# Modulation weights in two halves of longer rows, x transposed by a diagonal of its statistic, and a new order for the start

## The chip, the cores and the metric

The kernel runs on one core of one Trainium2 chip. Its time is the device time of one execution in microseconds (us); the time before is the median of three runs. The profile is that of one more execution.

## The reference, cut to what matters

One layer of a hybrid encoder works on 1024 prompt rows and 32 sample rows of width 1024. The change touches only how the layer begins: the modulation vectors, the normalised and modulated input h, and the first product of h with the weights w_in, whose first 512 columns are u.

```python
def layer(x, c, w_mod, b_mod, g_norm, w_in, ...):
    mod = silu(c) @ w_mod + b_mod                     # 1024 x 3072 weights
    shift, scale, gate = split(mod, 3)
    h = rms_norm(x, g_norm) * (1.0 + scale) + shift   # rsqrt(mean(x*x) + eps) per row
    z = h @ w_in
    u, zs, q, k, v, za, qi, ki, wi, gm = split(z, offs)
    # branch A: state space model over u; branch B: top-k sparse attention
    # merge with sigmoid gates, w_o, gate, residual, and a last rms_norm
```

## The kernel before, in words

The 1056 rows form three groups (0, 1, 2) of 256, 384 and 416 rows, and these are nine row tiles of up to 128 rows (indices 0 and 1; 2 to 4; 5 to 8, of which 8 holds the 32 sample rows). The width of 1024 is eight blocks of 128, the index k. The matrix multiply wants h transposed, that is, k on the partitions, and in two parts, hH and hL, a rounded high part and the rest. A weight has two parts too, wh and wl, and a product is three matmuls (`mm3`, lines 271 to 273): wh by hH, wh by hL, wl by hH.

The start of the kernel is written out by hand in the string `START`. Its tokens are steps, and each engine runs its instructions in the order in which the tokens issue them. What the tokens are:

- `sq i`, `ss i`, `sc i`: for row tile i, the squares and their sum on ACT (L214), the statistic rstd by DVE and POOL (L218, L219), and the scaling of the whole 128 x 1024 tile by rstd on DVE (`xscale`, L223).
- `mm j h`: block j (256 columns) of scale (h = 0) or shift (h = 1) of w_mod, multiplied with the activated c on PE into `pmrow` (`mod_mm`, L286). The eight k go to four strips of 32 partitions, two k to a strip.
- `row j h`: `pmrow` copied to `mrow` by ACT (L291). `co j h`: PE turns the row into columns in `pmod`, and sums the four strips by a selecting matrix (`mod_cols`, L296). `ap j`: three small DVE steps make scale and shift, `scl` and `sh`, for k = 2j and 2j + 1 (L302 to L304).
- `xt g k`: PE transposes block k of group g, one transposition for a row tile, into a bank of PSUM (`xtrans`, L231). Two banks take turns. `hf g k`: ACT applies `scl` and `sh` (L237, L239). `sp g k`: DVE makes hH and hL (L77, L78).
- `wl`: the parts of the u weights of a quarter q (128 columns): q 0 by ACT and DVE (L259, L264), q 1 by POOL in four pieces (L263, L264). `ub q g k`: the three matmuls of `mm3` for quarter q, group g, block k (`ublock`, the tile named pss in the trace). `ue`: the finished u goes to SBUF by ACT.
- `ld..`: loads that SP issues at this place. `aN`: N steps of a list of small DVE work for the state space model, which waits for free moments.

SP issues all large loads in order on one queue. Before, that is: row tiles 0 to 2, blocks 00 and 01 of w_mod, u weights of q 0, blocks 10 and 11, u weights of q 1, row tiles 3 to 5, the four other blocks of w_mod, row tiles 6 to 8, and then the weights of the next stage. A block of w_mod is 1 MiB and lies in HBM in rows of 1 KiB, a quarter of the u weights is 512 KiB in rows of 512 B, a row tile 512 KiB in rows of 4 KiB.

After the last `ub`, `ssm_consts` (L529, L533) makes the constants of the state space model. From there a planner with fixed costs lays out the jobs (tile pz) and the model's steps; it does not depend on measured time.

Of the kernel before, what the change touches and what calls it, by code (L numbers as in the profile page):

```python
# [7 lines left out]
F32 = mybir.dt.float32  # L8
# [4 lines left out]
ALU = mybir.AluOpType  # L13
# [3 lines left out]
T, TS, D = 1024, 32, 1024  # L17
# [4 lines left out]
KT = 8  # L22
# [8 lines left out]
WB = 5  # L31
# [14 lines left out]
MR, ML, YS, YW, HI, HG, JO, SF = (), 1, 10, 15, 0, 0, 8, (2, 2, 2, 1)  # L46
C_U, C_ZS, C_Q, C_K, C_V, C_ZA, C_QI, C_KI, C_GM = 0, 512, 1024, 1536, 2048, 2560, 3072, 3584, 3656
START = """
    sq0 ss0 sq1 sc0 ss1 sq2 sc1 ss2 sc2 mm00 srow ldw21 a13 xt00 row00 xt01 co00 mm01 ldw30 row01 wl00 co01
    ap0 mm10 ldw31 a2 hf00 row10 xt02 sp00 hf01 co10 sp01 xt03 mm11 ldx67 a6 wl10 ub000 row11 co11 sq3 ub100  # L50
    ap1 ub001 a1 ub101 hf02 ss3 a1 hf03 sp02 sq4 sp03 ub002 ub102 sq5 ss4 ub003 sc3 ub103 sc4 mm20 ldx8 ldz
    ss5 row20 a2 co20 sc5 a5 mm21 xt10 row21 xt11 hf10 co21 hf11 ap2 xt12 sp10 xt13 hf12 mm30 hf13 xt04 sp11
    row30 ub010 hf04 co30 sp12 xt05 xt14 hf05 ub110 sp13 hf14 mm31 sp04 xt15 row31 xt06 hf15 ub011 sp05 co31
    sq6 xt07 ap3 ub111 ub012 sp14 hf06 ub112 hf07 xt16 sp15 ub013 sq7 xt17 sp06 ub113 up hf16 ub004 sp07
    ub104 hf17 ub014 sp16 sq8 ub114 sp17 ub005 zs ub105 ss6 ub015 ss7 ss8 ub115 ub006 ub106 sc6 ub016 ub116
    sc7 ub007 sc8 ub107 ue00 ub017 ue10 a5 xt20 ue01 xt21 ub117 hf20 ue11 sp20 hf21 xt22 a1 ub020 hf22 xt23
    sp21 ub120 hf23 xt24 sp22 ub021 ub121 hf24 sp23 xt25 ub022 hf25 sp24 xt26 ub122 hf26 ub023 sp25 xt27
    ub123 sp26 hf27 ub024 ub124 sp27 ub025 ub125 ub026 ub126 ub027 ub127 ue02 ue12
    """
# [1 line left out]
GROW = [[n for g_, _, n in ROWS if g_ == g] for g in range(3)]  # L61


def body(nc, tc, I, O, dbg=None):
# [3 lines left out]
    te, ve, se, ge, sp = nc.tensor, nc.vector, nc.scalar, nc.gpsimd, nc.sync  # L68
# [88 lines left out]
    sc2 = cst.tile([128, 2, 8], F32)  # L157
# [3 lines left out]
    scP = cst.tile([128, 8, 32], F32, name="scP")  # L161
# [7 lines left out]
    bmod = pcol[:, 8:32]  # L169
# [5 lines left out]
    srow = pp.tile([80, 128], F32)  # L175
# [11 lines left out]
    pa = stA.enter_context(tc.tile_pool(name="pa", bufs=2, side="right", reuse_waits="tile"))  # L187
    scl = cst.tile([128, 8, 2], F32)
    sh = cst.tile([128, 8, 2], F32)
    nhalf = cst.tile([128, 9], F32)  # L190
    ge.memset(nhalf, -0.5)
    ss = cst.tile([128, 9], F32)
    rstd = cst.tile([128, 9], F32)
    XG, XW = {}, []

    def xload(i):
        g, r, n = ROWS[i]
        if i < 2:
            xt = stg.tile([128, D], F32, name="xt", tag="stg")
        elif i < 5:  # L200
            xt = XH[i // 4][:, D * (i == 3):D * (i == 3) + D]
        elif i == 5:
            xt = pa.tile([128, D], F32, name="xt", bufs=1)
        else:
            if i % 2 == 0:
                XW.append(pa.tile([128, 2, D], F32, name="xw", tag="wm", bufs=WB))
            xt = XW[-1][:, i % 2]
        load_rows(xt, g, r, n, sp)
        XG.setdefault(g, []).append(xt)

# [7 lines left out]
        ve.tensor_scalar(ss[:n, i:i + 1], ss[:n, i:i + 1], 1.0 / D, EPS, op0=ALU.mult, op1=ALU.add)  # L218
        ge.tensor_tensor(rstd[:n, i:i + 1], ss[:n, i:i + 1], nhalf[:n, i:i + 1], op=ALU.pow)  # L219

    def xscale(i):
        g, r, n = ROWS[i]
        ve.tensor_scalar_mul(XG[g][r][:n], XG[g][r][:n], rstd[:n, i:i + 1])  # L223

    PX, HX = {}, {}

    def xtrans(g, k):
        px = ps_z("px")
        PX[g, k] = px
        for r, n in enumerate(GROW[g]):  # L230
            te.transpose(px[:, r * 128:r * 128 + n], XG[g][r][:n, k * 128:(k + 1) * 128], idf[:n, :n])  # L231
# [16 lines left out]
    def wload(src, kt, n, pool=None):  # L248
        raw = (pool or wst).tile([128, kt, n], F32, tag="raw", name="raw", bufs=2)
        sp.dma_start(raw, src.rearrange("(k p) e -> p k e", p=128))  # L250
        return raw
# [21 lines left out]
        te.matmul(ps, wl, xh, start=False, stop=last)  # L273


    sel2 = pa.tile([128, 2], F32, name="sel2", bufs=1)
    WM, MR_ = {}, {}

    def mod_load(j, h):
        wm = WM[j, h] = pa.tile([128, 8, 256], F32, name="wm", tag="wm", bufs=WB)  # L280
        c = (1024, 0)[h] + 256 * j
        sp.dma_start(wm, w_mod[:, c:c + 256].rearrange("(k p) e -> p k e", p=128))

    def mod_mm(j, h):
        for k in range(8):
            te.matmul(pmrow[32 * (k % 4):32 * (k % 4) + 32, 256 * h:256 * h + 256], scP[:, k], WM[j, h][:, k],  # L286
                      start=k < 4, stop=k >= 4)

    def mod_row(j, h):
        MR_[j, h] = pa.tile([128, 256], F32, name="mrow", bufs=2)  # L290
        se.copy(MR_[j, h], pmrow[:, 256 * h:256 * h + 256])  # L291

    def mod_cols(j, h):
        for i in range(2):
            ch = (8, 0)[h] + 2 * j + i
            te.matmul(pmod[:, 2 * ch:2 * ch + 2], MR_[j, h][:, 128 * i:128 * i + 128], sel2, start=True, stop=True)  # L296

    def mod_apply(j):
        kk = slice(2 * j, 2 * j + 2)
        ks = slice(8 + 2 * j, 10 + 2 * j)  # L300
        bc2 = lambda ap: ap.unsqueeze(2).to_broadcast([128, 2, 2])
        ve.tensor_tensor(scl[:, kk], pm[:, ks], bc2(bmod[:, ks]), op=ALU.add)  # L302
        ve.tensor_tensor(scl[:, kk], scl[:, kk], bc2(gcol[:, kk]), op=ALU.mult)
        ve.tensor_tensor(sh[:, kk], pm[:, kk], bc2(bmod[:, kk]), op=ALU.add)  # L304

    scol = cst.tile([128, 5, 16], F32)
    are, aim, h0r, h0i, ldc = (scol[:, k] for k in range(5))
# [13 lines left out]
    now, ve = ve, Later(ve, todo)  # L321
# [149 lines left out]
    for k in range(7):  # L471
        n = 1 << k
# [39 lines left out]
    ve = now  # L512
# [62 lines left out]
    class Stream:  # L575
        STEP = 0.483

# [173 lines left out]
    mod_load(0, 0)
    mod_load(0, 1)
    uload(0)
    mod_load(1, 0)
    mod_load(1, 1)
    uload(1)
    for i in range(3, 6):
        xload(i)
    mod_load(2, 0)
    ve.tensor_add(sel2, idf[:, 0:2], idf[:, 32:34])  # L760
    for j in (64, 96):
        ve.tensor_add(sel2, sel2, idf[:, j:j + 2])
# [435 lines left out]
    for k in range(9):  # L1198
        n = 128 if k < 8 else 32
# [3 lines left out]
        o = (k % 4) * 72  # L1203
# [10 lines left out]
    for j in range(4):  # L1214
# [3 lines left out]
        for i in range(2, 9):  # L1218
            t0, m, k0, nk = (128 * i - B0[1], 128, 0, 128 * (i + 1)) if i < 8 else (T - B0[1], 32, 1024, 544)
            for e in range(2):  # L1220
                h = 2 * j + e
# [4 lines left out]
                for a in range(nb):  # L1226
                    c = slice(k0 + a * w_, k0 + (a + 1) * w_)
# [627 lines left out]
    ss2 = wo2.tile([128, 3, 9], F32, name="ss2")  # L1855
# [33 lines left out]
    for rows in ((0, 1, 2), (8,), (3,), (4,), (5,), (6,), (LAST,)):  # L1889
        xts = {}  # L1890
        for hcol in range(2):
            for i in rows:
                n = 128 if i < 8 else 32
# [3 lines left out]
                xt = xts[i]  # L1897
# [63 lines left out]
```

## Time and profile before

| | |
|---|---|
| median of three runs | 1007.07 us (1004.39 to 1008.39) |
| the profiled execution | 1005.85 us, its span 1003.9 us |
| PE (matmul) busy | 961.5 us, 96% of the span |
| DVE, ACT, POOL busy | 763.8, 525.2 and 234.3 us |
| loaded and stored | 124.24 MB, 124 GB/s over the span |

PE stands for the matrix engine, PEld for its weight loads, DVE for the vector engine, ACT for the scalar engine, POOL for GpSimd and SP for the engine that issues the loads. A row of the timeline gives the start, the duration and the engine, the line of the kernel, the tile that is written and those that are read, the shape and a count, and in square brackets how long the engine sat idle before it and what ended that. A row with a count (x16) is merged from several instructions that follow one another. Matmuls overlap, so what one costs is read from start to start. In the table by stages PEclk is the clock that was granted to the matrix engine, 1.00 being full speed.

### The profile page before, as it was taken

Reading aid. Unit: us, or ns where it says so; the run is one execution under the profiler, and the core shown is the slowest. Engines: PE = TensorE matmul, PEld = TensorE weight load, DVE = VectorE, ACT = ScalarE, POOL = GpSimd, SP = SyncE. Lnnn points to the kernel's source line nnn. Section 1 sums busy time; section 2 is a strip of 40 time slices with the busy share of each in tenths; the row PEclk is TensorE's granted clock in tenths of the full one; section 3 lists DMA queues with packets and bytes.
Section 4 is the critical chain, followed back from the end, with each engine's and each line's share of the span. In section 5 each row is a group of like instructions: output and inputs, shape, how many; then the busy total and the mean of one; then the engine's idle time right before and its main releaser. Section 6 shows DMA issues by size and latency. Waiting matters only on the chain. (4 is left out here: it accounts for less than half of the span.)

```text
span 1003.9 us, 16913 instructions
## 1 busy us (share of the span) xinstructions
PE 961.5 (96%) x6034; PEld 898.6 (90%) x6034; DVE 763.8 (76%) x1747; ACT 525.2 (52%) x1126; POOL 234.3 (23%) x443
## 2 busy tenths in 40 slices
PE   4999999999999999999999989999999999999997
PEld 2789999999898898998999979899898989998786
DVE  4669979994776878889999976676678786885543
ACT  3642234433655656858897266565576564443111
POOL 2202400000000024343323633333222222430000
PEclk8899999999999999999999999999999999999999
DMA  9922425437485222323323431322229503553311
GB/s 314 293 79 91 138 69 136 116 94 197 172 256 157 64 64 64 106 75 107 104 89 91 160 94 54 90 83 85 86 65 304 191 23 108 185 197 109 116 63 63
DMA packets 134255, 124.24 MB, mean 124 GB/s; under 512 B 20256, under 2 KB 114932, under 8 KB 134172
## 3 DMA queue, kind: packets, MB, share of 16 engines
q1 hardware_dynamic: 133232, 122.62, 40.1%
q8 instruction: 47, 0.77, 0.3%
q10 hardware_dynamic: 780, 0.52, 0.2%
q14 instruction: 36, 0.29, 0.1%
q0 software_dynamic: 160, 0.03, 0.0%
HBM read 87.74 MB, written 34.83 MB: 122 GB/s over the span
## 5 line engine op out<-in xcount | busy, mean ns | idle before, releaser
L271 PE MATMUL pz<-hH,wh 128*128 128x384 f32 (+4 forms) x744 | 253.1, 340 | 2.7 <-ACT tg L713 2.0
L272 PE MATMUL pz<-hL,wh 128*128 128x384 f32 (+4 forms) x744 | 244.9, 329 | 0.0
L273 PE MATMUL pz<-hH,wl 128*128 128x384 f32 (+4 forms) x744 | 244.9, 329 | 0.0
L264 POOL TENSOR_TENSOR wl<-raw,wh 128x256 fp32r<-128x256 f32 (+1 forms) x180 | 134.8, 778 | 121.4 <-ACT wh L259 111.0
L271 PEld LDWEIGHTS pz<-hH,wh 128*128 128x128 f32 (+1 forms) x744 | 139.4, 187 | 7.8 <-ACT tg L713 2.3
L272 PEld LDWEIGHTS pz<-hL,wh 128*128 128x128 f32 (+1 forms) x744 | 138.9, 187 | 1.7
L273 PEld LDWEIGHTS pz<-hH,wl 128*128 128x128 f32 (+1 forms) x744 | 138.6, 186 | 1.3
L1568 ACT ACTIVATE junkb<-sco,thr 128x768 bf16<-128x768 f32 (+3 forms) x128 | 96.7, 756 | 31.3 <-DVE thr L1650 20.5
L1570 DVE TENSOR_SCALAR_CACHE_REDUCE junk<-sco,thr 128x1024 bf16<-128x1024 f32 (+2 forms) x96 | 105.4, 1098 | 2.2
L271 PE MATMUL pss<-hH,wh 128*128 128x256 f32 (+2 forms) x304 | 97.8, 322 | 0.7 <-ACT tg L713 0.5
L272 PE MATMUL pss<-hL,wh 128*128 128x256 f32 (+2 forms) x304 | 95.8, 315 | 0.0
L273 PE MATMUL pss<-hH,wl 128*128 128x256 f32 (+2 forms) x304 | 95.5, 314 | 0.0
L263 POOL CAST wh<-raw 128x256 fp32r<-128x256 f32 x88 | 38.1, 473 | 178.2 <-PE pz L272 108.9
L1499 ACT CAST PH<-pt 128x512 fp32r<-128x512 f32 (+2 forms) x96 | 43.1, 483 | 37.6 <-PE pt L1497 34.1
L271 PEld LDWEIGHTS pss<-hH,wh 128*128 128x128 f32 x304 | 58.6, 193 | 3.6 <-issue 2.1
L1500 DVE TENSOR_TENSOR PL<-pt,PH 128x512 fp32r<-128x512 f32 (+2 forms) x96 | 50.4, 552 | 14.6 <-ACT PH L1499 13.7
L272 PEld LDWEIGHTS pss<-hL,wh 128*128 128x128 f32 x304 | 58.2, 191 | 0.3 <-DVE hL L78 0.2
L273 PEld LDWEIGHTS pss<-hH,wl 128*128 128x128 f32 x304 | 58.2, 192 | 0.0
L1236 DVE SCALAR_TENSOR_TENSOR sco<-rl,wi,sco 128x384 f32<-128x384 f32 (+6 forms) x49 | 46.8, 963 | 13.8 <-ACT rl L1231 12.6
L1231 ACT ACTIVATE rl<-pss 128x384 f32<-128x384 f32 (+6 forms) x56 | 40.9, 739 | 27.1 <-PE pss L1229 21.5
L1417 ACT ACTIVATE Sm<-Sm,mx 128x128 f32<-128x128 f32 (+8 forms) x68 | 52.7, 775 | 0.9 <-DVE mx L1410 0.8
L1932 PE MATMUL psm<-o,mL 128*128 128x512 f32 (+1 forms) x136 | 52.0, 382 | 0.0
(403 smaller groups left out, 2167.7 us busy)
## 6 DMA issues: line engine op xcount, KB each, us to landing
raw<-in_w_in SPq DMA_DIRECT2D x44, 512.0 KB
thD<-tg SPq DMA_DIRECT2D x16, 528.0 KB
wm<-in_w_mod SPq DMA_DIRECT2D x8, 1024.0 KB
m<-thD SPq DMA_DIRECT2D x8, 528.0 KB
tgl<-thD SPq DMA_DIRECT2D x8, 528.0 KB
rraw<-in_w_mod SPq DMA_DIRECT2D x4, 1024.0 KB
kd<-kd SPq DMA_DIRECT2D x32, 128.0 KB
xo<-in_x_prompt SPq DMA_DIRECT2D x8, 512.0 KB
```

Of the source, the lines that this page charges most:

```text
L264: leng.tensor_sub(wl[:, c], raw[:, c], f32(wh[:, c]))
L271: te.matmul(ps, wh, xh, start=first, stop=False)
L272: te.matmul(ps, wh, xl, start=False, stop=False)
L273: te.matmul(ps, wl, xh, start=False, stop=last)
L1231: se.activation(rl[:m, :nk].rearrange("p (b c) -> p b c", c=w_), pv, AF.Relu)
L1236: ve.scalar_tensor_tensor(sco[i][:m, :nk], rl[:m, :nk], w, sco[i][:m, :nk], op0=ALU.mult, op1=ALU.add)
L1417: se.activation(P, P, AF.Exp, scale=-1.0, bias=self.mx, accum_out=self.rs)
L1499: se.copy(PH[:, b0:b1_, oc], src)
L1500: ve.tensor_sub(PL[:, b0:b1_, oc], src, f32(PH[:, b0:b1_, oc]))
L1568: se.activation(junkb[:m, :nk], x[:m], AF.Sign, bias=t, accum_out=cnt[:m, k:k + 1])
L1570: ve.tensor_scalar(junk[:m, :nk], x[:m], t, None, op0=ALU.is_lt, op1=ALU.add, accum_out=cnt[:m, k:k + 1])
L1932: te.matmul(ps, ml, wh, start=False, stop=last)
```

## The change

- The columns of scale and shift are loaded in two halves instead of four quarters. A half (h) holds 512 columns of shift and the same 512 of scale, so that it serves four blocks k. It comes in four pieces (i), each of two k, by two loads with rows of 2 KiB in HBM. `mm h i` multiplies a piece: four matmuls over 512 columns (before, eight over 256), shift and scale of two k in the four strips. `row h`, `co h` and `ap h` then stand once for a half: two copies of 512 columns, two times four products with a selecting matrix of four columns (`sel4`), two times three DVE steps.
- x is no longer scaled. DVE makes for each row tile a 128 x 128 diagonal matrix of rstd, `dg i`, and PE multiplies block k of the row tile by it, a float32 matmul that transposes and scales at once, where a transposition by the identity stood. In group 0 one `xt` does two k, into the halves of one bank.
- The u weights of both quarters come in one load with rows of 1 KiB, into a buffer of the modulation weights. Row tiles 5 and 6 share a buffer, and 7 and 8.
- The loads stand in another order: row tiles 0 and 1, the first half of w_mod, the u weights, row tiles 2 to 4, the second half, row tiles 5 to 8.
- `START` is written anew. `mm1 i`, the products of the second half, stand among the other steps.

```diff
-    sq0 ss0 sq1 sc0 ss1 sq2 sc1 ss2 sc2 mm00 srow ldw21 a13 xt00 row00 xt01 co00 mm01 ldw30 row01 wl00 co01
...
+    sq0 ss0 sq1 dg0 ss1 dg1 mm00 srow ldw10 a13 xt00 mm01 ldw11 xt02 mm02 ldw12 mm03 ldw13 row0 co0 ap0 wl00 wl10 ldx56
...
-    def xscale(i):
+    DG = {}
+
+    def xdiag(i):
         g, r, n = ROWS[i]
-        ve.tensor_scalar_mul(XG[g][r][:n], XG[g][r][:n], rstd[:n, i:i + 1])
+        DG[g, r] = pa.tile([128, 128], F32, name="dg", bufs=5)
+        ve.tensor_scalar_mul(DG[g, r][:n, :n], idf[:n, :n], rstd[:n, i:i + 1])
...
     def xtrans(g, k):
-        px = ps_z("px")
-        PX[g, k] = px
-        for r, n in enumerate(GROW[g]):
-            te.transpose(px[:, r * 128:r * 128 + n], XG[g][r][:n, k * 128:(k + 1) * 128], idf[:n, :n])
+        pb = ps_z("px")
+        for j in range(2 if g == 0 else 1):
+            px = PX[g, k + j] = pb[:, 256 * j:]
+            for r, n in enumerate(GROW[g]):
+                te.matmul(px[:, r * 128:r * 128 + n], XG[g][r][:n, (k + j) * 128:(k + j + 1) * 128], DG[g, r][:n, :n],
+                          start=True, stop=True)
...
+    def mod_load(h, i):
+        wm = WM[h, i] = pa.tile([128, 2, 2, 512], F32, name="wm", tag="wm", bufs=WB)
+        for k in range(2):
+            sp.dma_start(wm[:, k], w_mod[256 * i + 128 * k:256 * i + 128 * k + 128, 0:2048]
+                         .rearrange("p (c a e) -> p c a e", c=2, a=2)[:, :, h])
+
+    def mod_mm(h, i):
+        for k in range(2):
+            for c in range(2):
+                o = 32 * (2 * k + c)
+                te.matmul(pmrow[o:o + 32, :], scP[:, 2 * i + k], WM[h, i][:, k, c], start=i == 0, stop=i == 3)
...
+    def uload():
+        t = pa.tile([128, KT, 256], F32, name="wm", tag="wm", bufs=WB)
+        sp.dma_start(t, w_in[:, C_U:C_U + 256].rearrange("(k p) e -> p k e", p=128))
...
+    xload(0)
+    xload(1)
+    for i in range(4):
+        mod_load(0, i)
+    uload()
+    for i in range(2, 5):
+        xload(i)
```

How the order of the instructions changes, at three places. First PE, from the first product with w_mod to the first blocks of u. Before:

```order
L286 MATMUL pmrow<-wm,scP 32x256 x8
L733 MATMUL pmod<-idf,srow 128x80
L231 MATMUL px<-idf,xt 128x128 x4
L296 MATMUL pmod<-sel_137,mrow 128x2 x2
L286 MATMUL pmrow<-wm,scP 32x256 x8
L296 MATMUL pmod<-sel_137,mrow 128x2 x2
L286 MATMUL pmrow<-wm,scP 32x256 x8
L231 MATMUL px<-idf,xt 128x128 x2
L296 MATMUL pmod<-sel_137,mrow 128x2 x2
L231 MATMUL px<-idf,xt 128x128 x2
L286 MATMUL pmrow<-wm,scP 32x256 x8
L271 MATMUL pss<-hH_84,wh 128x256
```

Four products of 1 MiB stand ahead of the first block of u here, with three of their turns into columns (pmod) between them; hH_84 is the high part of group 0. The same place now, with dg for the diagonals:

```order
L291 MATMUL pmrow<-wm,scP 32x512 x4
L740 MATMUL pmod<-idf,srow 128x80
L232 MATMUL px<-dg,xt 128x128 x4
L291 MATMUL pmrow<-wm,scP 32x512 x4
L232 MATMUL px<-dg,xt 128x128 x4
L291 MATMUL pmrow<-wm,scP 32x512 x8
L300 MATMUL pmod<-sel_137,mrow 128x4 x4
L273 MATMUL pss<-hH_84,wh 128x256
```

Again four products of 1 MiB come first, and the turn into columns stands once behind them all. Second PE, from the last product with w_mod on, where hH_82 is the high part of group 1. Before:

```order
L286 MATMUL pmrow<-wm,scP 32x256 x8
L231 MATMUL px<-idf,xh 128x128 x3
L231 MATMUL px<-idf,xt 128x128 x2
L271 MATMUL pss<-hH_82,wh 128x384
L272 MATMUL pss<-hL_83,wh 128x384
L273 MATMUL pss<-hH_82,wl 128x384
L296 MATMUL pmod<-sel_137,mrow 128x2 x2
L231 MATMUL px<-idf,xt 128x128 x2
```

And now:

```order
L291 MATMUL pmrow<-wm,scP 32x512 x4
L232 MATMUL px<-dg,xt 128x128 x8
L300 MATMUL pmod<-sel_137,mrow 128x4 x4
L273 MATMUL pss<-hH_82,wh 128x384
L274 MATMUL pss<-hL_83,wh 128x384
L275 MATMUL pss<-hH_82,wl 128x384
```

All four blocks k = 4 to 7 of group 0 are now transposed behind the last product, and one more block of group 1 (for q 1) stands between the turn into columns and the first block of group 0 that needs it. Third ACT, from the first copy of the modulation row on; wm in the second row is the load of the u weights. Now:

```order
L295 COPY mrow<-pmrow 128x512
L261 CAST wh<-wm 128x1024
L239 ACTIVATE hf<-px,sh,scl 128x256 x2
L211 ACTIVATE sq,ss<-xh 128x1024 x2
L239 ACTIVATE hf<-px,sh,scl 128x256
L211 ACTIVATE sq,ss<-xh 128x1024
L239 ACTIVATE hf<-px,sh,scl 128x256
```

The squares of row tiles 2 and 3 stand ahead of the third `hf`, that of tile 4 ahead of the fourth. Behind the start the orders of both kernels differ by swaps alone: single steps of the state space model stand some rows later or earlier among the jobs.

More of the change, by code (lines that the diff above doesn't have):

```diff
@@ L48 @@
 START = """
-    sq0 ss0 sq1 sc0 ss1 sq2 sc1 ss2 sc2 mm00 srow ldw21 a13 xt00 row00 xt01 co00 mm01 ldw30 row01 wl00 co01
[L50 to L56, printed above, removed]
+    sq0 ss0 sq1 dg0 ss1 dg1 mm00 srow ldw10 a13 xt00 mm01 ldw11 xt02 mm02 ldw12 mm03 ldw13 row0 co0 ap0 wl00 wl10 ldx56
+    hf00 sp00 hf01 sp01 ub000 sq2 ss2 ub001 sq3 hf02 sp02 ss3 sq4 hf03 sp03 ss4 dg2 dg3 dg4 ub100 ub101 mm10 ldx78 ldz
+    ub002 ub102 ub003 ub103 a6 xt10 hf10 sp10 xt11 hf11 sp11 mm11 xt12 hf12 sp12 ub010 ub110 mm12 xt13 hf13 sp13 ub011
+    ub111 ub012 ub112 a14 sq5 ss5 mm13 row1 xt04 sq6 ss6 xt06 co1 ub013 ub113 ap1 hf04 sp04 sq7 ss7 hf05 sp05 ub004 ub104
+    hf06 sp06 xt14 ub005 ub105 dg5 dg6 hf07 sp07 xt15 ub006 ub106 hf14 sp14 ub007 ub107 sq8 ss8 xt16 hf15 sp15 ub014 ub114
+    xt17 hf16 sp16 dg7 dg8 ub015 ub115 hf17 sp17 xt20 ub016 ub116 up zs ue00 ue10 xt21 ub017 ub117 hf20 sp20 ue01
+    hf21 ue11 xt22 a1 ub020 hf22 xt23
     sp21 ub120 hf23 xt24 sp22 ub021 ub121 hf24 sp23 xt25 ub022 hf25 sp24 xt26 ub122 hf26 ub023 sp25 xt27
@@ L201, in xload @@
             xt = XH[i // 4][:, D * (i == 3):D * (i == 3) + D]
-        elif i == 5:
-            xt = pa.tile([128, D], F32, name="xt", bufs=1)
         else:
-            if i % 2 == 0:
+            if i % 2 == 1:
                 XW.append(pa.tile([128, 2, D], F32, name="xw", tag="wm", bufs=WB))
-            xt = XW[-1][:, i % 2]
+            xt = XW[-1][:, 1 - i % 2]
         load_rows(xt, g, r, n, sp)
@@ L273, in mm3 @@
         te.matmul(ps, wl, xh, start=False, stop=last)
-    sel2 = pa.tile([128, 2], F32, name="sel2", bufs=1)
+    sel4 = pa.tile([128, 4], F32, name="sel4", bufs=1)
     WM, MR_ = {}, {}
[L279 to L302, printed above, removed]
+    def mod_load(h, i):
[3 more added lines that the diff above has]
+                         .rearrange("p (c a e) -> p c a e", c=2, a=2)[:, :, h])
@@ new lines, in mod_mm, with mod_row, mod_cols @@
+    def mod_mm(h, i):
[3 more added lines that the diff above has]
+                te.matmul(pmrow[o:o + 32, :], scP[:, 2 * i + k], WM[h, i][:, k, c], start=i == 0, stop=i == 3)
+    def mod_row(h):
+        MR_[h] = pa.tile([128, 512], F32, name="mrow", bufs=1)
+        se.copy(MR_[h], pmrow)
+    def mod_cols(h):
+        for i in range(4):
+            k = 4 * h + i
+            te.matmul(pmod[:, 4 * k:4 * k + 4], MR_[h][:, 128 * i:128 * i + 128], sel4, start=True, stop=True)
@@ L303, in mod_apply @@
+    def mod_apply(h):
+        kk = slice(4 * h, 4 * h + 4)
+        ks = slice(8 + 4 * h, 12 + 4 * h)
+        bc2 = lambda ap: ap.unsqueeze(2).to_broadcast([128, 4, 2])
+        ve.tensor_tensor(scl[:, kk], pm[:, kk, 1], bc2(bmod[:, ks]), op=ALU.add)
         ve.tensor_tensor(scl[:, kk], scl[:, kk], bc2(gcol[:, kk]), op=ALU.mult)
-        ve.tensor_tensor(sh[:, kk], pm[:, kk], bc2(bmod[:, kk]), op=ALU.add)
+        ve.tensor_tensor(sh[:, kk], pm[:, kk, 0], bc2(bmod[:, kk]), op=ALU.add)
     scol = cst.tile([128, 5, 16], F32)
@@ L724, in body @@
     raw = {}
-    def uload(q):
-        raw[q] = wload(w_in[:, C_U + 128 * q:C_U + 128 * q + 128], KT, 128)
+    def uload():
+        t = pa.tile([128, KT, 256], F32, name="wm", tag="wm", bufs=WB)
+        sp.dma_start(t, w_in[:, C_U:C_U + 256].rearrange("(k p) e -> p k e", p=128))
+        for q in range(2):
+            raw[q] = t[:, :, 128 * q:128 * q + 128]
     def uparts(q):
@@ L747, in load @@
             f()
-    for i in range(3):
-        xload(i)
[L751 to L762, printed above, removed]
+    xload(0)
+    xload(1)
+    for i in range(4):
+        mod_load(0, i)
+    uload()
+    for i in range(2, 5):
+        xload(i)
+    for c in range(2):
+        ve.tensor_add(sel4[:, 2 * c:2 * c + 2], idf[:, 32 * c:32 * c + 2], idf[:, 64 + 32 * c:66 + 32 * c])
     ve.memset(dl, 0.0)
     pmod, pmrow = ps_t("pmod"), ps_t("pmrow")
-    pm = pmod[:, 0:32].rearrange("p (k s) -> p k s", s=2)
-    STEP = dict(sq=xsquare, ss=xrstd, sc=xscale, mm=mod_mm, row=mod_row, co=mod_cols, ap=mod_apply, xt=xtrans,
+    pm = pmod[:, 0:32].rearrange("p (k c s) -> p k c s", c=2, s=2)
+    STEP = dict(sq=xsquare, ss=xrstd, dg=xdiag, mm=mod_mm, row=mod_row, co=mod_cols, ap=mod_apply, xt=xtrans,
                 hf=xmod, sp=xsplit, wl=lambda q, _: uparts(q), ub=ublock, srow=srows, zs=lambda: Z.split(0), up=utiles,
@@ L780, in body @@
             STEP[n](*(int(c) for c in t[len(n):]))
-        if t == "wl00":
+        if t == "mm00":
             ssm_shifts()
```

## The prediction

> **What bounds the kernel now.** I read the table by stages first, then PE's timeline of the start, then the rows of ACT and DVE that stand between two steps of PE. From the table of stages (length, busy time and instruction count of PE, PEld, DVE, ACT and POOL, then the granted clock, the DMA share and GB/s):
>
> ```profile
> core 0: us, PE busy (x) PEld busy (x) DVE busy (x) ACT busy (x) POOL busy (x), PEclk, DMA share, GB/s
> 6.64:18.97 12.33, 5.64 (x47) 3.59 (x47) 7.57 (x28) 4.07 (x8) 2.34 (x4) 0.97 1.10 344
> 14.00:16.00 2.00, 1.88 (x22) 1.20 (x20) 1.69 (x10) 0.06 (x1) 0.00 (x0) 1.00 1.15 316
> 32.00:34.00 2.00, 1.44 (x20) 0.78 (x12) 1.36 (x7) 0.37 (x1) 0.34 (x1) 1.00 1.09 348
> 38.00:40.00 2.00, 2.00 (x27) 1.50 (x19) 1.90 (x6) 1.37 (x3) 0.00 (x0) 1.00 1.08 390
> 18.10:31.75 13.65, 12.69 (x68) 8.82 (x68) 7.96 (x31) 6.04 (x12) 5.93 (x10) 0.50 1.09 356
> 41.06:69.16 28.10, 28.09 (x181) 24.91 (x181) 17.84 (x48) 16.37 (x34) 2.44 (x6) 1.00 0.40 73
> 71.00:130.00 59.00, 59.00 (x372) 58.88 (x373) 50.64 (x190) 14.75 (x28) 17.60 (x19) 1.00 0.43 127
> ```
>
> The start has two halves. Up to about 41 us the loads run without a gap at 316 to 390 GB/s, by the length of their rows (316 where the u weights with rows of 512 B are among them, 348 with rows of 1 KiB alone, 390 where row tiles with 4 KiB come in), and PE waits for them; from 18.10 to 31.75 its clock is at half. From 41.06 on PE is busy for 28.09 of 28.10 us, and for 59.00 of 59.00 us after it. So what PE has left to do when the last block of w_mod is there sets when the start ends, and a delay there is carried on one for one. PE's timeline gives the marks and the prices:
>
> ```profile
> 18.97 1.94 PE L286 MATMUL pmrow<-wm,scP 128*32 128x256 f32 x16 [1.99 <-DMA wm<-in_w_mod]
> ...
> 24.79 0.58 PE L271 MATMUL pss<-hH,wh 128*128 128x256 f32 x1
> ...
> 30.57 0.41 PE L272 MATMUL pss<-hL,wh 128*128 128x256 f32 x1
> 30.78 0.41 PE L273 MATMUL pss<-hH,wl 128*128 128x256 f32 x1
> ...
> 34.34 1.07 PE L286 MATMUL pmrow<-wm,scP 128*32 128x256 f32 x16 [0.40 <-DMA wm<-in_w_mod]
> 35.34 0.88 PE L231 MATMUL px<-idf,xh 128*128 128x128 f32 x6
> ...
> 39.49 0.50 PE L296 MATMUL pmod<-sel,mrow 128*128 128x2 f32 x4
> 39.85 0.42 PE L231 MATMUL px<-idf,xt 128*128 128x128 f32 x2
> ...
> 41.06 1.07 PE L286 MATMUL pmrow<-wm,scP 128*32 128x256 f32 x16
> ...
> 45.41 0.49 PE L231 MATMUL px<-idf,xh 128*128 128x128 f32 x3
> 45.65 0.42 PE L271 MATMUL pss<-hH,wh 128*128 128x384 f32 x1
> 45.91 0.34 PE L272 MATMUL pss<-hL,wh 128*128 128x384 f32 x1
> ...
> 49.38 0.28 PE L272 MATMUL pss<-hL,wh 128*128 128x256 f32 x1
> 49.49 0.28 PE L273 MATMUL pss<-hH,wl 128*128 128x256 f32 x1
> 49.61 0.34 PE L271 MATMUL pss<-hH,wh 128*128 128x384 f32 x1
> 49.79 0.34 PE L272 MATMUL pss<-hL,wh 128*128 128x384 f32 x1
> ...
> 54.25 0.33 PE L231 MATMUL px<-idf,xt 128*128 128x128 f32 x1
> ...
> 54.90 0.44 PE L271 MATMUL pss<-hH,wh 128*128 128x384 f32 x1
> ...
> 66.52 0.35 PE L272 MATMUL pss<-hL,wh 128*128 128x416 f32 x1
> 66.71 0.34 PE L273 MATMUL pss<-hH,wl 128*128 128x416 f32 x1
> ...
> 69.16 0.60 PE L529 MATMUL pt<-idf,cld 128*128 128x128 f32 x4
> ```
>
> From start to start a matmul of u costs 0.117, 0.175 and 0.188 us in groups 0, 1 and 2 (0.213 us for group 0 at half clock, 30.57 to 30.78), so a block of three 0.35, 0.525 and 0.565 us. A product of 1 MiB costs 1.0 us (34.34 to 35.34), a turn into columns 0.36 us (39.49 to 39.85). Three transpositions cost 0.24 us (45.41 to 45.65), 0.08 each, and the matmul behind them costs 0.26 instead of 0.175, 0.09 for the switch. Four with the one of 32 rows cost 0.65 us (54.25 to 54.90). The start ends at 69.16, where the constants begin.
>
> **The change part by part.**
>
> *The diagonal in place of the identity.* PE does a float32 matmul instead of a transposition. The state space model has such matmuls with nearly this shape:
>
> ```profile
> 136.15 2.07 PE L909 MATMUL pss<-Uq,Bc 128*128 128x133 f32 x16
> 137.97 0.42 PE L271 MATMUL pz<-hH,wh 128*128 128x384 f32 x1
> ```
>
> The loop of L909 issues eight matmuls, and sixteen records stand here: a float32 matmul runs as two passes, each with a weight load, where a transposition is one record (x3 for three row tiles). The eight take 1.82 us, 0.2275 each, or 0.114 a pass; the passes with only two columns in a turn into columns take 0.09 (0.36 for four), so the columns hardly count. I take 0.22 us for a row tile; the ends are 0.205 and 0.2275 us. For the piece of 32 rows, about 0.2 us before (0.65 less 0.24 and switches), I take 0.3, between 0.2 (no dearer) and 0.45 (two passes and their switches). The nine scalings of 128 x 1024 on DVE become 128 x 128. I count nothing for that: in the late stretch DVE is busy for 17.84 of 28.10 us, so it is not what PE waits for.
>
> *Loads.* Both kernels load row tiles 0 and 1 first, and ACT's squares of tile 1 show it there at 6.64 (row below). From there to 18.97, when the third block is there, 4 MiB come at 344 GB/s. For rows of 2 KiB there is no row; the bounds are 340 (all that this stretch mixes) and 390 GB/s, and I take 355, nearer to the 348 of 1 KiB since that row is w_mod itself. Then the first half (4.19 MB, 11.8 us) is there at 18.45, the u weights (3.1 us at 340) at 21.5, row tiles 2 to 4 (1.57 MB at 390, 4.0 us) at 25.6, and the pieces of the second half at 28.5, 31.5, 34.4 and 37.4. By the table of specifications in DMA: Bandwidth & Descriptors, a page of the Trainium skill, 512 B a row suffice for full rate; this trace does not agree (316, 348, 390). By that rule nothing lands sooner for its longer rows, the first piece of the second half comes at 29.8 instead of 28.5, and the sum below would be 1.3 us longer.
>
> *Up to the first block of u.* The rows of ACT and DVE:
>
> ```profile
> 6.64 1.06 ACT L214 ACTIVATE sq<-xt 128x1024 bf16<-128x1024 f32 x1 [0.45 <-DMA xt<-in_x_prompt]
> ...
> 38.88 0.37 ACT L291 COPY mrow<-pmrow 128x256 f32<-128x256 f32 x1 [0.41 <-PE pmrow L286]
> 39.22 0.56 ACT L237 ACTIVATE hf<-px,sh,scl 128x256 f32<-128x256 f32 x1
> ...
> 48.41 1.03 ACT L259 CAST wh<-raw 128x1024 fp32r<-128x1024 f32 x1
> ```
>
> ```profile
> 43.75 0.16 DVE L302 TENSOR_TENSOR scl<-pmod,pcol 128x4 f32<-128x4 f32 x1 [1.95 <-PE pmod L296]
> ...
> 44.09 0.35 DVE L77 CAST hH<-hf 128x384 fp32r<-128x384 f32 x1
> ...
> 46.48 0.29 DVE L77 CAST hH<-hf 128x256 fp32r<-128x256 f32 x1
> 46.80 0.42 DVE L78 TENSOR_TENSOR hL<-hf,hH 128x256 fp32r<-128x256 f32 x1
> ...
> 49.48 1.23 DVE L264 TENSOR_TENSOR wl<-raw,wh 128x1024 fp32r<-128x1024 f32 x1 [0.52 <-ACT wh L259]
> ```
>
> With the u weights at 21.5, ACT's cast (1.03) and DVE's subtraction (1.23) make their parts by 23.8, and hH and hL of block 0 (0.74) follow on DVE: PE's first block begins at about 24.6, against 24.79. So the early half buys no earlier start. Scale and shift are ready before (last product 18.45 to 19.5 or 20.3, copy 0.6, columns 0.9, three steps 0.34: 21.4 to 22.1). Four blocks of group 0 fill PE up to 27.2 at half clock. Then stands the product with the first piece of the second half, which lands at 28.5, and the blocks of k = 2 and 3 stand behind it in PE's order.
>
> *From 28.5 to the last product.* At full clock: three products 3.0, four blocks of group 0 1.4, four times three diagonals with their switch 4 x 0.75 = 3.0, six blocks of group 1 3.15; together 10.55 us. PE's clock was at half for 13.65 us before, though PE was busy for 12.69 of them; with PE idle from about 20 to 24.6 and 27.2 to 28.5 I let it rise at 33, which costs 2.25 us. The last product begins at 28.5 + 10.55 + 2.25 = 41.3, behind its load (37.4); before it began at 41.06. With the clock up at once it is 39.05, with half clock to 38 it is 43.8. By Part 4 of TensorE: Matmul & The Clock Gate, in the Trainium skill, transpositions do not count as PE's work for the clock as matmuls do; by that the diagonals would bring the clock up sooner, at best 2.25 us off the sum. The half clock over 12.69 busy us does not contradict it, but too few transpositions lie there to show it.
>
> *From the last product to the end.* Before, the 28.1 us are one product 1.0, one turn into columns 0.36, blocks of u 14 x 0.525 + 8 x 0.35 + 16 x 0.565 = 19.2, and so 7.5 for 37 transpositions, the eight small ones and their switches. Now:
> - the product 1.0, and the columns of four blocks, eight passes of 0.114, 0.9;
> - blocks of u: four of group 1 fewer, done ahead of the product, 17.1;
> - diagonals: 8 of group 0, 12 of group 1 and 24 of group 2, 44 x 0.22 = 9.7; 8 small ones 2.4; 13 switches 1.2: 13.3;
> - a new wait. The blocks of group 0 now need the turn into columns, three steps of DVE (0.34), `hf` (0.56) and the two steps of DVE (0.74), 1.64 and some 0.4 for the handovers; two blocks of group 1 cover 1.05. I take 1.0, with ends of 0.5 and 1.5. Behind the waiting matmul stands all of PE's work.
>
> Together 33.3 us. The start ends at 41.3 + 33.3 = 74.6 instead of 69.16: 5.4 us later. The fewer copies of ACT, the three DVE steps that fall away and SP's issues cost nothing and give nothing, since PE's own work covers them.
>
> **The rivals.**
> - *More of it is hidden.* Loads at 390 GB/s bring the first piece of the second half at 27.0, and the clock rises at 28.3; a row tile costs 0.205, a small one 0.2, the wait 0.5. The last product begins at 38.0, 31.3 us follow, the start ends at 69.3: 0.2 us later. The middle of this case is 2 us. For it speaks that three of these four are ends measured here.
> - *The clock stays down.* Half clock to 38, 1.5 us of wait, small pieces 0.45: 43.8 + 35.2 = 79.0, 9.8 us later. For it speaks that PE was busy for most of 13.65 us before without getting its clock.
> - *Faster.* A diagonal whose second pass costs nothing, like a transposition in a stream: at 0.11 for a tile and 0.2 for a small piece, with the loads of the first rival, 36.7 + 27.2 = 63.9, 5.3 us sooner. It decides below about 0.12 us for a tile. The sixteen records of L909 speak against it.
> - *Four times dearer.* At four times 0.11, 56 tiles from 28.5 on cost 12.3 us more than in my sum, 17.7 us later. The 0.2275 of L909 speaks against it. The Trainium skill has the rule behind this, in the Terms of TensorE: Matmul & The Clock Gate, where the transpose mode makes float32 four times faster; the trace shows about two.
>
> **How the numbers follow.** The profiled execution took 1005.85 us, so 5.4 us later is 1011.3; the median of the three runs is 1.2 us higher, and from it 1012.5. Between the two I say 1011.8. Half a per cent, about what a measurement of this kernel can tell from no change, is 5.0 us. Chances: the forecast (4 to 7 us later) 0.45, the clock that stays down (7 to 11) 0.18, more of it hidden (0 to 4) 0.28, faster 0.06, four times dearer 0.03. Slower by over 0.5% are six tenths of the forecast and the second and fourth rival, 0.48; faster by over 0.5% most of the third, 0.05; the rest, 0.47, is within. The range leaves out the third and fourth rival and the outer part of the two others: 1006.5 to 1017.
>
> **What would show it.** In the profile after: two records for a diagonal and 0.205 to 0.23 us for a row tile (below 0.12 I am wrong); the first block of u at 24 to 25.5; an idle PE ahead of the first product of the second half; the last product at 39 to 44; 32 to 35 us from there to the constants, which begin at 73 to 77; an idle PE ahead of the blocks k = 4 of group 0; behind it the same 59 busy us of 59. If the start ends at 69 or sooner, or if the delay is made up before 130 us, the sum is wrong.

## The result and the profile after

The changed kernel takes 1015.64 us (median; 1015.22 to 1016.85), the kernel before in the same comparison 1007.73 (1004.39 to 1009.27). The ratio is 1.0087, with a 95% interval of 1.0069 to 1.0104: slower, by 7.9 us between the medians, where 4.7 over the median shown was forecast. The profiled execution took 1015.34 us with a span of 1013.5, 9.6 us more than the span of 1003.9 before.

The start came out almost as forecast. The table by stages of the changed kernel (columns as in the prediction), cut at marks of its own start:

```profile
6.27:18.45 12.18, 10.62 (x50) 4.18 (x50) 4.27 (x21) 1.15 (x2) 1.89 (x3) 1.00 1.05 381
23.34:31.00 7.66, 6.96 (x27) 4.49 (x28) 6.00 (x19) 3.32 (x8) 5.07 (x8) 0.50 1.04 386
31.00:40.04 9.04, 9.04 (x65) 6.74 (x64) 3.84 (x10) 3.72 (x6) 0.00 (x0) 1.00 1.06 365
40.04:74.39 34.35, 33.92 (x223) 31.10 (x223) 18.85 (x59) 17.77 (x36) 2.41 (x7) 1.00 0.26 45
76.00:130.00 54.00, 54.00 (x341) 53.87 (x342) 50.65 (x192) 13.73 (x27) 16.81 (x19) 1.00 0.44 132
```

The loads run at 381 GB/s in the first stretch, where the kernel before had 344, and at 386 in the second, where it had 356. PE's clock is at half up to 31 us, and from the last product at 40.04 PE is busy for 33.92 of 34.35 us, up to the constants at 74.39. PE's timeline has the marks:

```profile
23.34 0.58 PE L273 MATMUL pss<-hH,wh 128*128 128x256 f32 x1 [2.95 <-DVE hH L76]
...
27.63 1.94 PE L291 MATMUL pmrow<-wm,scP 128*32 128x512 f32 x8
...
40.04 1.07 PE L291 MATMUL pmrow<-wm,scP 128*32 128x512 f32 x8
41.04 2.05 PE L232 MATMUL px<-dg,xt 128*128 128x128 f32 x16
42.93 0.95 PE L300 MATMUL pmod<-sel,mrow 128*128 128x4 f32 x8
...
44.71 0.34 PE L275 MATMUL pss<-hH,wl 128*128 128x384 f32 x1
45.41 0.39 PE L273 MATMUL pss<-hH,wh 128*128 128x256 f32 x1 [0.36 <-DVE hH L76]
45.86 0.38 PE L274 MATMUL pss<-hL,wh 128*128 128x256 f32 x1
46.08 0.29 PE L275 MATMUL pss<-hH,wl 128*128 128x256 f32 x1
...
50.18 0.83 PE L232 MATMUL px<-dg,xh 128*128 128x128 f32 x6
50.76 0.42 PE L273 MATMUL pss<-hH,wh 128*128 128x384 f32 x1
...
53.62 1.16 PE L232 MATMUL px<-dg,xw 128*128 128x128 f32 x8
54.72 0.44 PE L273 MATMUL pss<-hH,wh 128*128 128x384 f32 x1
...
74.39 0.60 PE L533 MATMUL pt<-idf,cld 128*128 128x128 f32 x4
```

Each diagonal leaves two records (x16 for eight row tiles, x6 for three). The start ends 5.23 us later than before (74.39 against 69.16). But the span grew by 9.6: from the constants to the end stand 939.1 us where there were 934.7. So 4.4 us came in behind the start, where the prediction had put nothing. The table of PE's waits (wait in all, how often, the longest) has one entry of over 1 us behind the start that the kernel before lacks, and the stage from 200 to 300 us, before and after, shows its place:

```profile
PE pss L972 <- DVE HS L954: 3.2, 1, 3.2
```

```profile
200.00:300.00 100.00, 98.58 (x626) 95.42 (x624) 72.79 (x119) 46.10 (x77) 1.36 (x22) 1.00 0.60 179
```

```profile
200.00:300.00 100.00, 95.42 (x600) 92.54 (x601) 74.06 (x125) 44.17 (x72) 0.66 (x4) 0.98 0.55 161
```

PE is busy for 3.16 us less between 200 and 300 us, and part of that time its clock is lower. This is one wait, in the last quarter of the state space model, where PE multiplies the states HS that DVE's scan has made. PE's row before, its row after, and the stage right behind that:

```profile
229.12 0.49 PE L970 MATMUL pss<-HS,G 128*128 128x133 f32 x2
```

```profile
239.22 0.77 PE L972 MATMUL pss<-HS,G 128*128 128x133 f32 x2 [3.17 <-DVE HS L954]
```

```profile
239.00:243.00 4.00, 3.78 (x18) 3.78 (x19) 2.82 (x7) 0.38 (x1) 0.14 (x2) 0.57 0.02 4
```

The wait of 3.17 us is followed by a clock at half: four microseconds at a mean of 0.57 lose 1.7 us. Wait and clock are 4.9 us. A row of PE further on, of the same matmul before and after, bears this out:

```profile
342.19 0.31 PE L1228 MATMUL pss<-kiH,qis 128*32 128x272 f32 x1 [1.48 <-ACT rl L1231]
```

```profile
352.24 0.31 PE L1230 MATMUL pss<-kiH,qis 128*32 128x272 f32 x1 [1.48 <-ACT rl L1233]
```

Here the changed kernel is 10.05 us behind, 4.8 more than the 5.23 of the start. At the end it is 9.6 us behind, so some 0.4 us are made up in between, and the 4.4 us are accounted for. By the Trainium skill (TensorE: Matmul & The Clock Gate, Part 1), the clock needs about 3.4 us of sustained work to come back; this trace agrees, since a mean of 0.57 over four microseconds is half clock for 3.4 of them. The start of the same trace shows no such short rise: from 23.34 on PE is busy for 6.96 of 7.66 us, and the clock stays at half.

Why HS is late is read from DVE's timeline: before, and after:

```profile
214.12 0.69 DVE L864 TENSOR_TENSOR G<-G,e 128x512 f32<-128x512 f32 x1
214.73 1.26 DVE L978 SCALAR_TENSOR_TENSOR a<-a,Yq 128x1064 f32<-128x1064 f32 x1
215.90 0.70 DVE L925 TENSOR_TENSOR w<-vv,TCt 128x532 f32<-128x532 f32 x1
...
220.01 1.22 DVE L264 TENSOR_TENSOR wl<-raw,wh 128x1024 fp32r<-128x1024 f32 x1
...
228.36 0.71 DVE L952 TENSOR_TENSOR HS<-gr,gi 64x536 f32<-64x536 f32 x1
```

```profile
220.82 0.69 DVE L866 TENSOR_TENSOR G<-G,e 128x512 f32<-128x512 f32 x1
224.27 1.23 DVE L266 TENSOR_TENSOR wl<-raw,wh 128x1024 fp32r<-128x1024 f32 x1 [2.75 <-ACT wh L261]
225.41 1.26 DVE L980 SCALAR_TENSOR_TENSOR a<-a,Yq 128x1064 f32<-128x1064 f32 x1
226.59 0.70 DVE L927 TENSOR_TENSOR w<-vv,TCt 128x532 f32<-128x532 f32 x1
...
234.94 0.75 DVE L266 TENSOR_TENSOR wl<-raw,wh 128x576 fp32r<-128x576 f32 x1
...
238.45 0.71 DVE L954 TENSOR_TENSOR HS<-gr,gi 64x536 f32<-64x536 f32 x1
```

Before, DVE did the last gelu step (a) and six steps of the scan, and then the low part wl of the next weight. Now wl stands ahead of them all, and DVE sits idle for 2.75 us until ACT has made wh. A second wl, of 576 columns, stood behind HS (at 232.95); now it too stands ahead, and the step behind it begins 0.67 us later for it (235.61). From the last G to HS it takes 17.63 us instead of 14.24, and these two, 3.42 us, are the difference. The scan's steps begin at 226.59 instead of 215.90, 10.7 us later where the start gave 5.2, and HS begins 10.1 us later. This order comes from the planner, which lays out the weights' parts against the model's steps; and it was moved by the small list: the new `START` takes 34 steps of it (`a13 a6 a14 a1`), the old one 36. The rest of the list is done behind the start, a turn at a time with the planner's rows, so that two steps more shift the rows of the weights against those of the model.

### The profile page after: what moved, and what is told of

It is laid out like the page before. It is cut to its first block, busy times and chain, and to the rows that moved or that the text cites. A ratio compares the mean times of both kernels' runs of the same rounds, so it can differ in the third digit from the quotient of the medians.

```text
span 1013.5 us, 16899 instructions
## 1 busy us (share of the span) xinstructions
PE 970.3 (96%) x6026; PEld 904.3 (89%) x6026; DVE 760.5 (75%) x1740; ACT 522.9 (52%) x1120; POOL 235.4 (23%) x443
## 5 line engine op out<-in xcount | busy, mean ns | idle before, releaser
L266 POOL TENSOR_TENSOR wl<-raw,wh 128x256 fp32r<-128x256 f32 (+1 forms) x176 | 131.7, 778 | 122.0 <-ACT wh L261 111.9
L1233 ACT ACTIVATE rl<-pss 128x384 f32<-128x384 f32 (+6 forms) x56 | 41.0, 738 | 28.5 <-PE pss L1231 20.5
```

Of the source, the lines that this page charges most:

```text
L266: leng.tensor_sub(wl[:, c], raw[:, c], f32(wh[:, c]))
L1233: se.activation(rl[:m, :nk].rearrange("p (b c) -> p b c", c=w_), pv, AF.Relu)
```

## The experiments

Theory A is that story: the two missing steps of the list, through the order behind the start, cost some 4 us, and the start the rest. The other theories (the price of the diagonal, of the longer rows) are named in the expectations.

**1. The list's steps put back into the changed kernel.** Behind the start the orders are then those of the kernel before, row for row.

```diff
-    hf21 ue11 xt22 a1 ub020 hf22 xt23
+    hf21 ue11 xt22 a3 ub020 hf22 xt23
```

> The changed kernel with two more steps of the small DVE list inside START (a1 becomes a3 near its end), so that all orders behind START are those of the kernel before, row for row. Theory A, a delay of two parts: the start itself costs 5.2 us (constants at 74.4 instead of 69.2), and two list steps fewer inside START shifted the planner's rows so that the state space scan of the last quarter came late (PE idle 3.2 us ahead of HS, then about 1 us at half clock). By A the constants still begin at 74.2 to 74.7, no idle PE over 1 us stands at the HS matmuls, and the time is 5.2 us (4 to 6.5) over the kernel before, ratio 1.004 to 1.0065. Theory B, the late start itself makes the scan late: nothing changes, the wait stays and the time is 7.5 to 9 us over the kernel before.

Measured: 1010.4 us against 1007.5 for the kernel before on the same chip, ratio 1.003 (1.0019 to 1.0042). The stage of the wait, and the end of the start:

```profile
200.00:300.00 100.00, 98.60 (x626) 95.45 (x625) 76.42 (x129) 46.70 (x78) 1.35 (x22) 1.00 0.59 172
```

```profile
74.33 0.60 PE L533 MATMUL pt<-idf,cld 128*128 128x128 f32 x4
```

The start ends where it did, PE's busy time from 200 to 300 us is again that of the kernel before (98.60 against 98.58), at full clock, and 5 us of the loss are gone. The mechanism of A holds, and rival B fell with it: with the same late start the wait is gone. A's size for the start does not hold. The remaining 2.9 us, a ratio of 1.003, lie below the 4 to 6.5 us and 1.004 to 1.0065 that it gave (see experiment 6).

**2. The kernel before with two steps of the list fewer.** Its start is otherwise untouched.

```diff
-    sc7 ub007 sc8 ub107 ue00 ub017 ue10 a5 xt20 ue01 xt21 ub117 hf20 ue11 sp20 hf21 xt22 a1 ub020 hf22 xt23
+    sc7 ub007 sc8 ub107 ue00 ub017 ue10 a3 xt20 ue01 xt21 ub117 hf20 ue11 sp20 hf21 xt22 a1 ub020 hf22 xt23
```

> The kernel before with two list steps fewer inside START (one a5 becomes a3), so that all orders behind START are those of the changed kernel, row for row. By A the start is as before (constants at 69.0 to 69.5) and the wait ahead of the HS matmuls of the last quarter appears: 3 us idle and 1 us at half clock, 3.5 to 5 us over the kernel before, ratio 1.0035 to 1.005. By B nothing happens: within 1 us of the kernel before.

Measured: 1011.58 us, ratio 1.0049 (1.0032 to 1.0067). Its constants begin at 69.39, as before, and its PE shows the wait without any of the change:

```profile
234.26 0.49 PE L970 MATMUL pss<-HS,G 128*128 128x133 f32 x2 [3.03 <-DVE HS L952]
```

```profile
200.00:300.00 100.00, 95.40 (x597) 92.39 (x596) 73.17 (x125) 46.01 (x76) 1.35 (x22) 0.98 0.58 166
```

One number in the string, two small steps of DVE, costs half a per cent of the kernel, 165 us later. Together with experiment 1 (1.003) this makes 1.0079, and the whole change 1.0087: the two parts add up within their intervals.

**3. The diagonal undone.** Experiment 1, but DVE scales x again and PE transposes by the identity; loads, halves and order stay as changed.

```diff
-        ve.tensor_scalar_mul(DG[g, r][:n, :n], idf[:n, :n], rstd[:n, i:i + 1])
+        ve.tensor_scalar_mul(XG[g][r][:n], XG[g][r][:n], rstd[:n, i:i + 1])
...
-                te.matmul(px[:, r * 128:r * 128 + n], XG[g][r][:n, (k + j) * 128:(k + j + 1) * 128], DG[g, r][:n, :n],
-                          start=True, stop=True)
+                te.transpose(px[:, r * 128:r * 128 + n], XG[g][r][:n, (k + j) * 128:(k + j + 1) * 128], idf[:n, :n])
```

> As the first kernel of this call, with the diagonal undone: x is scaled on DVE and transposed by the identity, in the new order and with the new loads. Theory C, the start is late because a float32 matmul takes two passes where a transposition takes one: from the last product to the constants PE has some 6 us less (13 groups of transpositions cost 7.4 instead of 14.3), so 27 to 29 us instead of 34.3; the constants begin at 67 to 69.5, and the time is within 2 us of the kernel before, ratio 0.998 to 1.002. Theory D, the halves and the order of the loads are what delays the start: the constants stay at 73 to 75, 4 to 6 us over the kernel before.

Measured: 1004.55 us, ratio 0.9967 (0.9954 to 0.998): faster than both kernels. PE's timeline:

```profile
38.21 1.07 PE L289 MATMUL pmrow<-wm,scP 128*32 128x512 f32 x8
39.21 1.09 PE L231 MATMUL px<-idf,xt 128*128 128x128 f32 x8
40.14 0.95 PE L298 MATMUL pmod<-sel,mrow 128*128 128x4 f32 x8
...
52.99 0.66 PE L231 MATMUL px<-idf,xw 128*128 128x128 f32 x4
53.58 0.45 PE L271 MATMUL pss<-hH,wh 128*128 128x384 f32 x1
...
68.37 0.60 PE L531 MATMUL pt<-idf,cld 128*128 128x128 f32 x4
```

Eight row tiles cost 0.93 us instead of 1.89, a group of four 0.59 instead of 1.10. The start ends 5.96 us earlier than in experiment 1, and the medians stand 5.85 apart: as far as one profile of each can tell, the start's delay is carried one for one here. Of the 5.96 us, 4.15 lie behind the last product (30.16 us instead of 34.31), at full clock. The other 1.81 lie ahead of it, and there the clock also came up sooner in this execution (half up to 29.7 us, in experiment 1 up to 31.2), so they are not all the diagonal's. Theory D falls. C is right in its mechanism and missed two numbers: 30.16 us where it gave 27 to 29, with three waits for DVE among them (experiment 5), and a ratio below its 0.998. The diagonal alone takes more than the halves and the new order give (0.8 us at the start's end, 69.16 against 68.37; 3.0 us between the medians). Run once more beside experiment 5 (below), the same kernel gave 0.997 (0.9955 to 0.9984).

> e3 once more, beside e5 on the same chip. If e3 is faster than the kernel before, its ratio is again 0.995 to 0.998; the rival, that the first measurement was chance, gives 0.998 to 1.002.

**4. The rows of w_mod cut back to 1 KiB**, with all else as in experiment 1: each load is made as two of half the columns.

```diff
-            sp.dma_start(wm[:, k], w_mod[256 * i + 128 * k:256 * i + 128 * k + 128, 0:2048]
-                         .rearrange("p (c a e) -> p c a e", c=2, a=2)[:, :, h])
+            for e in range(2):
+                sp.dma_start(wm[:, k, :, 256 * e:256 * e + 256], w_mod[256 * i + 128 * k:256 * i + 128 * k + 128, 0:2048]
+                             .rearrange("p (c a e) -> p c a e", c=2, a=2)[:, :, h, 256 * e:256 * e + 256])
```

> As the first kernel of this call, with each load of w_mod cut into two that have rows of 1 KiB in HBM instead of 2 KiB. Theory E, PE and not the loads paces the start from the first block of u on: the loads fall from about 380 to about 350 GB/s, the second half lands 2 to 3 us later and still ahead of its products but for the first, and the constants begin within 1 us of the first kernel's, ratio to it 1.000. Rival F, the longer rows carry the start: the constants come 2 to 3 us later.

Measured: 1012.54 us, ratio 1.0044 (1.0027 to 1.0061). The median is 2.1 us above that of experiment 1, but the two intervals overlap. Stages up to 18 us, of experiment 1 and then of this one, and the end of its start:

```profile
2.00:18.00 16.00, 9.90 (x51) 3.50 (x51) 5.04 (x26) 3.89 (x7) 4.25 (x9) 1.00 1.02 362
```

```profile
2.00:18.00 16.00, 10.01 (x47) 3.79 (x47) 4.94 (x26) 3.89 (x7) 4.26 (x9) 1.00 1.04 337
```

```profile
74.11 0.60 PE L534 MATMUL pt<-idf,cld 128*128 128x128 f32 x4
```

Longer rows do load faster, 362 against 337 GB/s, with the DMA engines busy throughout in both (a share of 1.02 and 1.04), so the 512 B that the Trainium skill names as enough for full rate (DMA: Bandwidth & Descriptors, Specifications) are not enough here. The cut also doubles the number of loads, and rows and number were not tried apart. At the start's end little of it is left, 74.11 against 74.33, where PE is the bound. Chance may have a part in that: the first block of u came 1.1 us later (24.36 against 23.23), but the clock was at half up to 29.3 us instead of 31.2. Half of the 1.9 us is 0.9, so with the same clock the end would be at about 75.0, an estimate; that is 0.7 us for the rate, within the 1 us of theory E and far from the 2 to 3 of F.

**5. Experiment 3 with its gaps covered.** Its PE still waited 0.49, 0.30 and 0.32 us for DVE behind the last product. Two blocks of group 1 go behind the turn into columns, and the scalings of tiles 5 to 8 stand one step later or earlier.

```diff
-    ub111 ub012 ub112 a14 sq5 ss5 mm13 row1 xt04 sq6 ss6 xt06 co1 ub013 ub113 ap1 hf04 ...
-    hf06 sp06 xt14 ub005 ub105 dg5 dg6 hf07 sp07 xt15 ...
-    xt17 hf16 sp16 dg7 dg8 ub015 ...
+    ub111 a14 sq5 ss5 mm13 row1 xt04 sq6 ss6 xt06 co1 ub012 ub112 ub013 ub113 ap1 hf04 ...
+    hf06 sp06 xt14 ub005 ub105 hf07 sp07 dg5 dg6 xt15 ...
+    xt17 dg7 dg8 hf16 sp16 ub015 ...
```

> e3 with three steps moved in START: two blocks of group 1 now stand behind the turn into columns instead of ahead of the last product, and the scalings of row tiles 5 to 8 one step later or earlier on DVE. Theory C2: the start of e3 is bounded by PE, so each idle gap of its chain that is covered is worth its length: the gaps of 0.49, 0.30 and 0.32 us ahead of blocks of group 0 and the last transposition go, the constants begin 0.8 to 1.3 us earlier than e3's 68.37 (67.1 to 67.6), and the median falls by about 1 us, to 1003 to 1004. Rival: the gaps only move, because DVE or the loads set the rate (the last product now stands 1.05 us earlier and waits for its load); then the constants begin at 68.1 to 68.7 and the time is that of e3.

Measured: 1003.86 us, ratio 0.9967 (0.9955 to 0.9978), beside 1005.26 for experiment 3 in the same comparison; the two intervals lie on each other, so the gain isn't shown. The constants begin at 67.65, at the edge of what C2 gave (67.1 to 67.6). The last product, the constants and the clock, of this kernel (first fences) and of experiment 3's second run:

```profile
37.67 1.07 PE L289 MATMUL pmrow<-wm,scP 128*32 128x512 f32 x8
...
67.65 0.60 PE L531 MATMUL pt<-idf,cld 128*128 128x128 f32 x4
```

```profile
28.00:30.00 2.00, 2.00 (x9) 0.20 (x9) 1.86 (x5) 0.00 (x0) 1.74 (x2) 0.50 1.05 387
30.00:32.00 2.00, 2.00 (x18) 2.00 (x15) 1.48 (x7) 0.00 (x0) 0.00 (x0) 0.83 1.04 385
```

```profile
37.42 1.06 PE L289 MATMUL pmrow<-wm,scP 128*32 128x512 f32 x8
...
67.71 0.60 PE L531 MATMUL pt<-idf,cld 128*128 128x128 f32 x4
```

```profile
28.00:30.00 2.00, 2.00 (x16) 0.98 (x9) 1.82 (x5) 0.00 (x0) 1.08 (x2) 0.84 1.04 386
```

The gaps are gone but for one of 0.15 us: 29.98 us from the last product to the constants, though 1.05 us of blocks were moved into this stretch, against 30.29. What was saved, 1.36 us, doesn't show at the end, because in this execution the clock rose 2 us later (half up to 30.7 instead of 28.6, by the means of the rows), which is worth about 1 us, an estimate: half of the difference.

**6. Second profiles** of the kernel before and of experiment 1, since the medians differ by 2.9 us and the starts by 5.2.

> The kernel before, a second profile. Open is why e1 begins its constants 5.2 us later than the kernel before and yet its median is only 3.0 us above. Theory G: the first profile of the kernel before is a good execution; in others PE waits for HS in the last quarter of the scan, where nothing is to spare, or its clock dips; then this profile shows a wait or a stage with a clock below 1.00 worth 1 to 3 us that the first did not have, and a longer span (1005 to 1007). Rival H: the start itself is different from one execution to the next; then the constants begin 1 us or more away from 69.16.

> e1, a second profile. By theory G its start stands where it stood (constants at 74.1 to 74.6) and the time behind it is 0 to 2 us shorter than in its first profile (935.7 us); by rival H the constants begin 1 us or more away from 74.33.

Measured: 1005.52 us with the constants at 69.38, and 1013.9 us with the constants at 75.10. Neither theory, as it was put, accounts for the 2 us: the second profile of the kernel before has no new wait, its time behind the constants is 934.3 us (934.7 in the first), and that of experiment 1 is 937.0 (935.7), not shorter. The starts differ by 0.2 and 0.8 us between two executions. Both profiled executions of the kernel before are 1.7 to 2 us below its median, those of experiment 1 are 1.5 to 3.5 above.

What G asked for, a dip of the clock, is there all the same, in experiment 1. In each of the ten profiles PE sits idle for 1.5 us (the row at 342.19 above) and, some 113 us later, for 2.0. Behind one of the two the clock falls to half for 3.4 us in some executions. First the first profile of experiment 1 (with 0.91 in the four microseconds ahead of this row), then its second (0.92 ahead):

```profile
462.00:466.00 4.00, 4.00 (x17) 3.87 (x16) 3.75 (x10) 3.78 (x10) 0.00 (x0) 0.67 0.95 248
```

```profile
350.00:354.00 4.00, 4.00 (x18) 4.00 (x17) 3.02 (x4) 1.24 (x3) 0.00 (x0) 0.65 0.28 84
```

Such a dip loses about 1.7 us. Five of the ten profiles have one (both of experiment 1, those of 2 and 5, and the second of 3), neither of the kernel before does. From the constants to the end the four profiles without it and without the long wait at HS take 934.2 to 934.7 us, the four with it alone 934.5 to 937.0. Dips in other executions of the kernel before would put its median above its two profiles. But what it does there isn't in any trace, and this stays open.

## Why the prediction was wrong, by its own steps

- **First block of u**, 24.6 forecast, 23.34 measured: the loads ran at 381 GB/s up to 18.45 us where 355 were taken, so the u weights came sooner (ACT's cast of them begins at 20.57, forecast 21.5). For the same reason no idle PE stands ahead of the product at 27.63 (forecast: a wait up to 28.5).
- **The clock** was at half to 31 instead of 33. With the sooner loads that puts the last product at 40.04 instead of 41.3, still within the range that was given (39 to 44).
- **The diagonals.** A row tile cost 0.236 us where eight follow one another (41.04 to 42.93) and 0.19 to 0.23 in a group of three (0.19 from 50.18 to 50.76), around the 0.22 taken. The group of three with the piece of 32 rows was mis-sized: 1.10 us (53.62 to 54.72) where 3 x 0.22 + 0.3 = 0.96 were taken. Eight such groups are 1.1 us. The other terms came out near what was taken, and so it took 34.35 us from the last product to the constants instead of 33.3.
- **The new wait** ahead of block k = 4 of group 0 is there, and its size was right. The bracket shows 0.36 us, but read from start to start it is more, since the second matmul waits too, for hL (ready on DVE at 45.80): from 44.71 to 46.08 it takes 1.37 us, where the prices 0.175 and two times 0.117 make 0.41. So 0.96 us were lost, and 1.0 was taken.
- **The end of the start:** 5.23 us later, 5.4 forecast; two misses of about 1 us, one on each side of the last product, cancelled. That the sum came so close is luck.
- **The step that failed** is the next one: "a delay there is carried on one for one", that is, nothing happens behind the start. It rested on 59.00 busy us of 59.00 up to 130 us, which came true (54.00 of 54.00), and on the remark ahead of it that the orders behind the start differ "by swaps alone". The swaps were seen and not priced. Two of them put parts wl of weights ahead of the scan's steps, and the missing term is 3.2 us of wait and 1.7 us of half clock at 239 us; experiments 1 and 2 measured it as 5.2 and 4.1 us between medians (the first from two comparisons). That it is these swaps of wl which make the wait, and not others of the same reordering, is read from DVE's rows; it wasn't tried by itself.
- **The small list** was not in the sum at all: that its steps fell from 36 to 34 can be counted in `START`.
- The rivals were all about the start's own size. None was about what an unchanged part does when its order moves; the time came out within the range of 1006.5 to 1017, but at the side where the clock that stays down stood, for another reason, and so by luck.

## What to carry to other kernels

When a change alters a count that a later scheduler starts from, compare the order of the whole program, find the handovers with nothing to spare (a handover is where one engine takes what another has just made; here HS, ready at 228.36 + 0.71 = 229.07 us and taken by PE at 229.12), and price each swap ahead of them. A transposition that also scales is no free fusion: in float32 it turned one record into two on the engine that bounds the stage (x8 into x16 for eight row tiles), and here the separate scaling on DVE was 5.85 us cheaper. Experiment 3 is the version to keep, at 0.9967 of the time before; experiment 5 is not told apart from it.

## What the hardware showed unexpectedly

- An idle of 3.2 us on PE in the middle of the program cost half as much again: about 3.4 us at half clock behind it, 1.7 us. Idles of 1.5 and 2.0 us were followed by the same 3.4 us in five of ten profiles and by none in the others, of the same kernel too (experiment 3).
- When the clock comes up at the start varies between executions of one kernel: half up to 29.7 and 28.6 us in the two profiles of experiment 3, 31.2 and 31.9 us in those of experiment 1. By the half that is lost, 1 us of it is 0.5 us at the end of the start, an estimate.
- A float32 matmul with 32 rows and columns cost 0.4 to 0.5 us where it ends a group (1.10 us with it, 0.58 to 0.69 for three row tiles alone), more than two row tiles of 0.19.
